# Mixer activations normalised in place, gates taken out of PSUM by ScalarE, and four of sixteen gate tiles as three products

## The chip, the cores and the metric

The kernel runs on one core of one Trainium2 chip. The metric is the device time of one execution in microseconds (us), as the median of several runs, and lower is better. In the profile the engines are PE (TensorE, the matrix unit), PEld (its weight loads), DVE (VectorE), ACT (ScalarE), POOL (GpSimd) and SP (the queue that issues most weight transfers). Every engine works through its own list of instructions in order; semaphores hold an instruction back until what it reads is there and what it overwrites has been read.

## The reference: what is computed

A trunk of two layers over 272 tokens (16 meta tokens and 256 others) with 1024 features, all in float32. Each layer is a mixer followed by a PEER block.

```python
h = _rmsnorm(x, mix_g)
z = h @ w_in                       # 1024 -> 3488 columns, the last 2048 of them gate logits
u = conv_in[..., :512] * sigmoid(conv_in[..., 512:])
u = silu(_layernorm(_causal_depthwise_conv(u, conv_w, conv_b)))     # 31 taps, 512 channels
y_conv = u @ w_conv_out
...                                # low-rank attention, 8 heads, chunk-causal: o
y_mla = o @ w_mla_out
gates = sigmoid(gate_logits)
merged = gates[..., :1024] * y_conv + gates[..., 1024:] * y_mla
h = x + merged @ w_out
```

The PEER block picks, for each token and each of 8 heads, 16 of 16384 experts by two top-16 searches, and adds `sum(gelu(u_e . h) * w_e * v_e)`. The second layer needs no outputs for the meta tokens, so most of its tiles are 256 columns wide where those of the first are 272.

## The kernel before

Activations lie transposed: features on the 128 partitions, tokens along the free dimension, 8 blocks of 128 features. Weights stream from HBM through a ring of four 1 MB buffers (`wraw`); each holds two tiles, and a tile is the 1024x128 weights of one output block. `next_w` goes one tile on and lets SP issue the transfer three buffers ahead; `peek_w(n)` looks at a tile that comes n tiles later. The order of the instructions on each engine is the order in which the Python code calls them. Nothing reorders them, so where a call stands in the program decides what it queues behind.

One mixer goes through these stages:

- **Input tiles.** `ztile` multiplies one tile of `w_in` with `xg`, the activations times the norm's gain. A tile is 8 float32 matmuls, which PE executes as 16 instructions. The factor `rs` of the RMS norm (one number per token) is not in `xg`; VectorE multiplies it into every result on its way out of PSUM. PSUM has three buffers named `z`, used in turn. Three tiles for the low-rank inputs and one for the rope keys come first, then eight for the convolution (loop over `c`, two tiles each, `za` and `zb`), then sixteen gate tiles (loop over `i`, 0 to 15).
- **Attention and convolution beside them.** `attention()` and `conv2()` are generators. Each loop advances them by `next(att)` and by `taps`, so that scores, softmax, transposes and mixes stand between the tiles on PE, and convolution taps (one VectorE instruction each) fill VectorE. The list `TAPS` says how many taps each gate tile brings. Channel block 0 has 21 of its 31 taps done by ScalarE and added up by POOL transfers.
- **Gates.** VectorE writes `z * rs` into `g0` or `g1` (L792). ScalarE applies the sigmoid in place later (L787), once the last exponential of the softmax is behind (`vt["exp"]`), which saves changes of ScalarE's function table.
- **LayerNorm.** When all taps are done, `layernorm()` is created and advanced by two steps a tile: two sums over PE, a reciprocal square root of eleven VectorE instructions, a sigmoid and a scaling on ScalarE for each of four blocks (L723, L724), then the products `u`.
- **Output tiles as three products.** The matrices `w_mla`, `w_conv`, `w_out` and part of `wq` are multiplied in another number format (float32r). ScalarE rounds a weight tile to a high part (`high`, L666), VectorE subtracts it from the weights to get a low part (`low`, L676), and `three` multiplies high x high, low x high and high x low: three instructions for each of 8 blocks, 24 a tile. `half_tile` makes the two halves of a tile of `w_mla` or `w_conv` (12 instructions each). The high and low parts reuse buffers that the mixer no longer needs: `wuq`, `seln` with `upad`, `kh`, `acc` with `sqa`, chosen by the part's number in `high`.
- **Merge and output.** `merge` multiplies the conv halves with their gates, adds the attention halves, and splits the sum in a high and a low part (`xh`, `xl`); eight tiles of `w_out` follow, then the sixteen tiles of `wq`, and the PEER block.

In the stage between, the tile numbers are: gate tiles 0 to 15, then parts 0 to 3 (the four tiles of `w_mla`), 4 to 7 (`w_conv`), 8 to 15 (`w_out`).

Of the kernel before, what the change touches and what calls it, by code (L numbers as in the profile page):

```python
# [20 lines left out]
T = 272  # L21
# [5 lines left out]
TAPS = [4, 4, 7, 7] + [9] * 12  # L27
KD = 21
SCALE = 96 ** -0.5
# [6 lines left out]
        "kh", "wuq", "seln", "upad", "acc", "sqa", "g0", "g1"}  # L36
# [13 lines left out]
def trunk_kernel(ctx: ExitStack, tc: tile.TileContext, a: dict, out: bass.AP, dbg=None, stop=None):  # L50
# [146 lines left out]
    for l in range(NL):  # L197
# [8 lines left out]
        rpool = rp.enter_context(tc.tile_pool(name=f"route{l}", bufs=1, side="right"))  # L206
# [28 lines left out]
        wuq = mp.tile([128, 2, 8 * 128], F32, name="wuq")  # L235
        wuk = mp.tile([128, 512], F32, name="wuk")
        wuv = mp.tile([128, 512], F32, name="wuv")
        qh, kh = pp.tile([128, 8, T], F32, name="xh"), mp.tile([128, 8, T], F32, name="kh")
        rope = mp.tile([128, T], F32, name="rope")
# [28 lines left out]
        nc.sync.dma_start(wuq, a["w_uq"][l])  # L268
# [37 lines left out]
        cq = mp.tile([128, 3, T], F32, name="cq")  # L306
# [14 lines left out]
        def attention():  # L321
# [15 lines left out]
            def qhead(h):  # L337
                pq = aps()
                for c in range(2):
                    mm(pq[:, :TQ], wuq[:, c, h * 128:(h + 1) * 128], cq[:, c, t0:], c == 0, c == 1)  # L340
# [229 lines left out]
            for x in range(11):  # L570
                p = x // 2
                if x % 2 == 0:
# [7 lines left out]
                    if p < 4:  # L580
                        softmax(p, ps)
                    yield
                else:
# [64 lines left out]

        def high(i, n):

            w_ = peek_w(n)
            x = {19: 3, 21: 4, 23: 1, 25: 2}.get(i, i % 3)
            if x == 0:
                t_ = mp.tile([128, 2, 1024], F32, name="wuq")
                hi, lo = t_[:, 0], t_[:, 1]
            elif x == 1:
                hi = mp.tile([128, 1024], F32, name="seln")
                lo = mp.tile([128, 1208], F32, name="upad")[:, 0:1024]
            elif i == 2 or x > 2:
                t_ = mp.tile([128, 8 * T], F32, name="kh" if x < 4 else "sq", tag="kh" if x < 4 else "sq")  # L660
                hi, lo = t_[:, 0:1024], t_[:, 1024:2048]
            else:
                hi = mp.tile([128, 4 * T], F32, name="acc")[:, 0:1024]
                lo = mp.tile([128, 4 * T], F32, name="sqa")[:, 0:1024]
            parts[i] = hi.bitcast(F32R), lo.bitcast(F32R), w_
            S.activation(parts[i][0], w_, AF.Copy)  # L666
            if i > 20:
                S.activation(parts[i][1], w_, AF.Copy, scale=-1.0)

        def low(i):  # L670

            hi, lo, w_ = parts[i]
            if i > 20:
# [874 lines left out]
```

## Time and profile before

| | |
|---|---|
| median of 3 runs | 1734.21 us (1732.22 to 1735.2) |
| profiled execution, its own time | 1733.18 us |
| its span, first to last instruction | 1731.4 us |
| PE busy | 1694.2 us (98% of the span), 11995 matmuls |
| DVE, ACT, POOL busy | 1148.1, 559.4, 306.5 us |
| mixer of layer 1 up to its last merge product | from the start to about 193 us |
| mixer of layer 2 | begins at 884.94 us |

A row of the timeline gives start, duration, engine, line, operation, output and inputs, shapes and a count, and in brackets an idle time before it with what ended it. A row with a count runs from the start of its first to the end of its last instruction; because matmuls are pipelined, a row's end overlaps the next row's start, and the distance from start to start is what a stretch takes. The list of waits gives the total, the number and the longest. A window row gives the busy time and, in brackets, the number of instructions of each engine, then the clock granted to PE (PEclk, 1.00 is full), the share of the transfer engines and GB/s. Line numbers up to the first changed line agree in both kernels; later ones of the changed kernel are higher.

### The profile page before, as it was taken

What the parts mean: (1) busy time and instruction counts of PE and PEld (TensorE: products, weight loads), DVE (VectorE), ACT (ScalarE), POOL (GpSimd) and SP (SyncE); (2) the same over time, 40 slices, a digit from 0 to 9 for tenths busy, and PEclk for the clock granted to TensorE, in tenths of its full rate; (3) what the DMA queues carried; (4) which work ended last, traced back from release to release, by engine and by line L of the source; (5) the groups of instructions that cost most, each with busy time, mean ns of one, the idle gap of its engine ahead of it and who ended that gap; (6) DMA issues with size and microseconds to landing.
All of it is one profiled execution on the core that took longest, in us unless ns stands there. A gap on an engine that the chain in (4) does not pass through costs nothing.

```text
span 1731.4 us, 30489 instructions
## 1 busy us (share of the span) xinstructions
PE 1694.2 (98%) x11995; PEld 1603.0 (93%) x11995; DVE 1148.1 (66%) x2987; ACT 559.4 (32%) x1596; POOL 306.5 (18%) x352
## 2 busy tenths in 40 slices
PE   9998999999999999999999989999999999999998
PEld 7677999989999999999986879999999999999998
DVE  6686888887888544443456868897888885333332
ACT  3455633434554111000024546333355441000000
POOL 0000022222112222233200100212221113222120
PEclk9999999999999999999999999999999999999999
DMA  6353686999999999999962546969999999999995
GB/s 238 108 146 122 219 266 238 369 382 418 420 420 416 421 421 421 421 420 416 418 251 98 134 131 232 288 273 365 396 425 424 424 418 415 389 387 391 397 391 206
DMA packets 85231, 568.50 MB, mean 328 GB/s; under 512 B 9560, under 2 KB 14872, under 8 KB 17624
## 3 DMA queue, kind: packets, MB, share of 16 engines
q1 hardware_dynamic: 49488, 338.54, 49.5%
q0 software_dynamic: 34880, 227.41, 33.9%
q8 instruction: 94, 1.54, 0.4%
q10 hardware_dynamic: 720, 0.60, 0.1%
q14 instruction: 49, 0.40, 0.1%
HBM read 556.18 MB, written 1.05 MB: 322 GB/s over the span
## 4 chain that ended last, share of the span: by engine, by line
PE 75%; issue 9%; DMA 8%; DVE 4%; POOL 2%; ACT 2%; POOLq 0%; SPq 0%; ACTq 0%; DVEq 0%
PE po L58 27%; PE z L58 20%; PE A L58 20%; DMA wraw<-vn 6%; PE aps L58 4%; DMA gb<-uv,iww 2%; POOL gb L1314 2%; PE wp L58 1%; PE sc L58 1%; PE xp L58 0%; DVE gb L1339 0%; DVE va L1325 0%; DVE upad L676 0%; DVE rq_w L179 0%; DVE rq_w L178 0%
## 5 line engine op out<-in xcount | busy, mean ns | idle before, releaser
L58 PE MATMUL A<-xh,wraw 128*128 128x160 f32 x3776 | 534.8, 301 | 1.2 <-ACT idxT L944 1.2
L58 PEld LDWEIGHTS A<-xh,wraw 128*128 128x128 f32 x3776 | 517.7, 191 | 1.6 <-issue 1.6
L1339 DVE SCALAR_TENSOR_TENSOR gb<-gb,xr 128x1024 f32<-128x1024 f32 x208 | 254.5, 1223 | 397.1 <-DMA gb<-uv,iww 396.7
L1314 POOL DMA_INDIRECT gb<-uv,iww x208 | 223.7, 1076 | 526.5 <-DVE va L1325 377.0
L58 PE MATMUL po<-Xh,wraw 128*128 128x160 f32 x2080 | 286.9, 300 | 4.1 <-DMA wraw<-vn 3.4
L58 PEld LDWEIGHTS po<-Xh,wraw 128*128 128x128 f32 x2080 | 283.1, 190 | 6.7 <-DMA wraw<-vn 5.4
L58 PE MATMUL po<-X,wraw 128*128 128x160 f32 x2016 | 277.8, 300 | 4.7 <-DMA wraw<-vn 2.5
L58 PEld LDWEIGHTS po<-X,wraw 128*128 128x128 f32 x2016 | 274.3, 190 | 7.7 <-DMA wraw<-vn 5.1
L58 PE MATMUL z<-xg,wraw 128*128 128x272 f32 (+2 forms) x1152 | 268.7, 391 | 0.0
L1325 DVE SCALAR_TENSOR_TENSOR va<-gb,am,va 128x1024 f32<-128x1024 f32 x203 | 259.6, 1279 | 4.0 <-ACT am L1350 3.7
L58 PEld LDWEIGHTS z<-xg,wraw 128*128 128x128 f32 (+1 forms) x1152 | 211.5, 189 | 46.0 <-issue 7.6
L1349 ACT ACTIVATE am<-am 128x1 f32<-128x1 f32 x208 | 41.3, 199 | 591.3 <-DVE gb L1339 591.2
L1253 ACT ACTIVATE ohA<-ohE,wlo 128x128 f16<-128x128 f16 x320 | 105.2, 429 | 6.4 <-DVE ohE L1250 5.7
L1313 POOL COPY warm<-wraw 1x1 f32<-1x1 f32 x86 | 40.7, 473 | 320.8 <-DMA wraw<-vn 320.8
L626 DVE SCALAR_TENSOR_TENSOR acc<-upad,cols,acc 128x272 f32<-128x272 f32 (+1 forms) x198 | 84.2, 484 | 0.2
L1264 ACT ACTIVATE Xh<-wp 128x260 f32<-128x260 f32 (+18 forms) x80 | 25.0, 313 | 126.5 <-DVE Xh L1261 116.6
L1350 ACT ACTIVATE am<-am,iww 128x1 f32<-128x1 f32 x208 | 61.3, 295 | 6.8
L1250 DVE TENSOR_TENSOR ohE<-ioh,idxT 128x512 f16<-128x512 f16 x160 | 60.1, 416 | 0.0
L638 POOL DMA_DIRECT2D part<-cp x12 | 13.2, 1102 | 249.4 <-ACT cp L635 249.4
L58 PE MATMUL wp<-ohE,ohA 128*128 128x128 f16 x640 | 51.4, 219 | 2.5 <-DVE ohA L1251 2.5
L58 PEld LDWEIGHTS <-ohA 128*128 128x128 f16 x640 | 43.3, 97 | 7.8 <-DVE ohA L1251 3.2
L58 PE MATMUL A<-xh,we 128*128 128x160 f32 x320 | 45.3, 299 | 0.0
(401 smaller groups left out, 1750.2 us busy)
## 6 DMA issues: line engine op xcount, KB each, us to landing
wraw<-vn SPq DMA_DIRECT2D x128, 1024.0 KB, 10.6
wraw<-u SPq DMA_DIRECT2D x118, 1024.0 KB, 10.3
wraw<-w_in SPq DMA_DIRECT2D x27, 1024.0 KB, 6.2
wraw<-wq SPq DMA_DIRECT2D x16, 1024.0 KB, 5.0
we<-u SPq DMA_DIRECT2D x10, 1024.0 KB, 8.8
wraw<-w_out SPq DMA_DIRECT2D x8, 1024.0 KB, 5.3
wraw<-w_mla SPq DMA_DIRECT2D x4, 1024.0 KB, 4.7
wraw<-w_conv SPq DMA_DIRECT2D x4, 1024.0 KB, 4.8
```

Source lines behind the costliest of these rows:

```text
L58: PE.matmul(o, l, r, start=start, stop=stop, skip_group_check=True)
L626: V.scalar_tensor_tensor(acc[:, c, t0:], u_, weight(c, k), acc[:, c, t0:], op0=OP.mult, op1=OP.add)
L638: G.dma_start(part[:, :, t0:], u_[:, :, t0:], accum_op=OP.add)
L1250: V.tensor_tensor(E[q], ioh[:, None].to_broadcast(full), pairs(q, b), op=OP.is_equal)
L1253: S.activation(A_[1][:, t // 2, :, t % 2], E[0][:, t // 2, :, t % 2], AF.Copy, scale=wlo[:, 4 * b + t:4 * b + t + 1])
L1264: S.activation(x_, p[:, :, a:b].rearrange("p t j -> p j t"), AF.Copy, scale=1.0 / WS)
L1313: G.tensor_copy(warm[0:1], state["w"][0:1, 0:1])
L1314: G.indirect_dma_start(out=g_, out_offset=None, in_=a[f"uv{l}"], in_offset=bass.IndirectOffsetOnAxis(ap=iww[i].bitcast(I32)[:, m // 16, 0, ...
L1325: V.scalar_tensor_tensor(vac[i], r, m_, vac[i], op0=OP.mult, op1=OP.add)
L1339: V.scalar_tensor_tensor(u_, u_, 1.0, xrs[i], op0=OP.mult, op1=OP.mult, accum_out=m_)
L1349: S.activation(m_, m_, AF.Gelu_apprx_tanh)
L1350: S.activation(m_, m_, AF.Copy, scale=iww[i][:, m // 16, 1, m % 16:m % 16 + 1])
```

## The change

Six things change in the mixer of each layer.

1. Between the two tiles of `c == 2`, VectorE multiplies `rs` into all eight blocks of `xg`, in place. From then on no result needs the factor: `zb` of block 2 goes straight to ScalarE's sigmoid, `za` of block 3 is read in PSUM by the product with the gate, and the sixteen gate tiles have no VectorE instruction.
2. ScalarE takes each gate out of PSUM: with the sigmoid at once if the last exponential is behind, otherwise as a copy whose sigmoid comes later from the list `todo`. `vt["exp"]` is set where the last softmax is issued, two tiles sooner.
3. `xg` is split into a high part `xnh` (ScalarE) and a low part `xnl` (VectorE), and gate tiles 12 to 15 (`TPG`) become three products. Their weight parts are `g12` to `g15`.
4. The parts of `w_mla` are prepared sooner: 0 at gate tile 13, 1 at tile 14, 2 and 3 at tile 15, and 4 and 5 after the first two half tiles. `kinds` lays out the buffers; `wuq` is split into `wq0` and `wq1`, and the buffer `xh`, free between the scores and the merge, is used too.
5. The taps are spread otherwise (`TAPS`), and the LayerNorm advances by 2, 4, 0 and 1 steps at the tiles after its creation, all between the two attention steps and what follows.
6. Small weights and `cq` share one buffer `un`, which `xnl` takes over; the pool of the routing is opened after the mixer.

```diff
-TAPS = [4, 4, 7, 7] + [9] * 12
+TAPS = [6, 6, 7, 8] + [8] * 12
+TPG = (12, 13, 14, 15)
...
+        kinds = {"g12": ("wq0", "x0"), "g13": ("wq1", "x1"), "g14": "s", "g15": "k", 0: "w", 1: "x", 2: "s", 3: "k",
+                 19: "k", 21: "q", 23: "s", 25: "a", 27: "w"}
...
+            x = kinds.get(i) or "was"[(i - 4) % 3]
...
             za = ztile(0)
             next(att, None)
             next(att, None)
+            if c == 2:
+                for k in range(8):
+                    V.tensor_mul(xg[:, k], xg[:, k], rs)
             zb = ztile(0)
...
-            V.tensor_mul(bz, zb, rs)
-            V.tensor_mul(az, za, rs)
-            S.activation(bz, bz, AF.Sigmoid)
+            if c < 2:
+                V.tensor_mul(bz, zb, rs)
+            if c < 3:
+                V.tensor_mul(az, za, rs)
+            S.activation(bz, bz if c < 2 else zb, AF.Sigmoid)
             next(att, None)
-            V.tensor_mul(upad[:, c, KW - 1:], az, bz)
-            taps((0, 0, 8, 4)[c], 2 if c >= 1 else 0, (1, 2, 3)[:max(c, 1)])
+            V.tensor_mul(upad[:, c, KW - 1:], az if c < 3 else za, bz)
+            if c == 2:
+                xnh = big("uk", [8, T], F32R)
+                xnl = mp.tile([128, 8, T], F32, name="un").bitcast(F32R)
+                for k in range(8):
+                    S.activation(xnh[:, k, t0:], xg[:, k, t0:], AF.Copy)
+                    V.tensor_tensor(xnl[:, k, t0:], xg[:, k, t0:], xnh[:, k, t0:].bitcast(F32), op=OP.subtract)
+            taps((0, 0, 8, 6)[c], 2 if c >= 1 else 0, (1, 2, 3)[:max(c, 1)])
...
         for i in range(16):
-            z = ztile(t0)
-            V.tensor_mul(gt[i // 8][:, i % 8, t0:], z, rs[:, t0:])
+            if i in TPG:
+                next_w()
+                z = zp.tile([128, 512], F32, name="z", bufs=3)[:, :TQ]
+                three(f"g{i}", z, (xnh, xnl), 0, range(8), 0, 7)
+            else:
+                z = ztile(t0)
+            ex = "exp" in vt
+            S.activation(gt[i // 8][:, i % 8, t0:], z, AF.Sigmoid if ex else AF.Copy)
+            if not ex:
+                todo.append(i)
+            new = [f"g{i + 2}"] if i + 2 in TPG else []
+            ns = [1] if new else []
+            for j in {13: (0,), 14: (1,), 15: (2, 3)}.get(i, ()):
+                new.append(j)
+                ns.append(15 - i + j)
+            for j, n in zip(new, ns):
+                high(j, n)
+            if i == 13:
+                for j in new:
+                    low(j)
+                new = []
...
-                next(ln, None)
                 next(att, None)
-                next(ln, None)
                 next(att, None)
-            if "exp" in vt:
-                gates(min(i + 1, ng[0] + 2))
-            if i == 14:
-                high(0, 1)
-                low(0)
-        gates(16)
-        high(1, 1)
+                for _ in range((2, 4, 0, 1)[lnk]):
+                    next(ln, None)
+                lnk += 1
+            for j in new:
+                low(j)
+            if ex:
+                gates(1)
...
-        low(1)
-        high(2, 2)
-        low(2)
         for i in range(4):
             ps = half_tile(i, oo)
-            if i == 2:
+            if i == 1:
                 run_all(ln)
-            if i < 3:
-                high(i + 3, 2)
-                low(i + 3)
+            if i < 2:
+                high(i + 4, 3)
             next(ln, None)
             for f in range(2):
                 V.tensor_mul(gt[1][:, 2 * i + f, t0:], gt[1][:, 2 * i + f, t0:], ps[f])
             next(ln, None)
-        run_all(ln)
+            if i < 2:
+                low(i + 4)
+            gates(2 if i < 2 else 4)
```

How the instructions stand now is shown at three places of the first layer. The first is ScalarE's list from the LayerNorm's last sigmoid (L723, L724) to the first products of `u` (L729). L666 is `high`, into the buffer named at its left. Before:

```order
L723 ACTIVATE sqa<-acc,cols_61 128x272
L724 ACTIVATE acc<-acc,cols_61 128x272
L787 ACTIVATE g_596<-g_596 128x272 x6
L666 ACTIVATE seln<-wraw 128x1024
L666 ACTIVATE kh<-wraw 128x1024
L666 ACTIVATE wuq<-wraw 128x1024
L729 ACTIVATE uk<-acc 128x272 x4
```

and now (L825 takes a gate out of PSUM, L814 is the later sigmoid, L676 is `high`, L733 and L734 are the LayerNorm's sigmoid and scaling):

```order
L825 ACTIVATE g_616<-z 128x272
L676 ACTIVATE kh<-wraw 128x1024
L676 ACTIVATE wq_1232<-wraw 128x1024
L814 ACTIVATE g_615<-g_615 128x272
L825 ACTIVATE g_616<-z 128x272
L676 ACTIVATE xh<-wraw 128x1024
L814 ACTIVATE g_615<-g_615 128x272
L825 ACTIVATE g_616<-z 128x272
L676 ACTIVATE seln<-wraw 128x1024
L676 ACTIVATE kh<-wraw 128x1024
L733 ACTIVATE sqa<-acc,cols_61 128x272
L734 ACTIVATE acc<-acc,cols_61 128x272
```

The high parts of the attention tiles stood behind the LayerNorm's eight instructions and six gate sigmoids; they now stand ahead of all of these.

The second place is VectorE's list at the end of the convolution (L626 are taps, L644 adds ScalarE's part, L686 is `low`, L713 and L716 begin the LayerNorm). This stretch now reads:

```order
L686 TENSOR_TENSOR xh<-wraw,wq_1080 128x1024
L626 SCALAR_TENSOR_TENSOR acc<-upad,cols_61,acc 128x272 x4
L531 TENSOR_TENSOR sq<-aps,sq 128x256
L626 SCALAR_TENSOR_TENSOR acc<-upad,cols_61,acc 128x272 x2
L644 TENSOR_TENSOR acc<-acc,part 128x272 x3
L686 TENSOR_TENSOR xh<-wraw,wq_1133 128x1024
L713 TENSOR_SCALAR kr<-aps 128x272
L716 TENSOR_TENSOR acc<-acc,kr 128x272 x4
L686 TENSOR_TENSOR upad<-wraw,seln 128x1024
L686 TENSOR_TENSOR kh<-wraw,kh 128x1024
L686 TENSOR_TENSOR wq_1233<-wraw,wq_1232 128x1024
L723 TENSOR_SCALAR rq_x<-aps 128x272
```

Here the low parts of the four gate tiles and of part 0 have come in: one ahead of the last taps, one behind the convolution, three between the LayerNorm's two halves. The two gate results of the stretch that VectorE took out of PSUM (L792) are gone.

The third place is VectorE's list where the LayerNorm ends and the conv products begin. L830, now L870, multiplies an attention half with its gate and so frees a PSUM buffer. Before:

```order
L720 TENSOR_TENSOR acc<-acc,rq_yl 128x272 x4
L676 TENSOR_TENSOR upad<-wraw,seln 128x1024
L676 TENSOR_TENSOR kh<-wraw,kh 128x1024
L676 TENSOR_TENSOR wuq<-wraw,wuq 128x1024
L728 TENSOR_TENSOR acc<-acc,sqa 128x272 x4
L731 TENSOR_TENSOR uk<-acc,uk 128x272 x4
L830 TENSOR_TENSOR g_596<-g_596,z 128x272
```

and now:

```order
L730 TENSOR_TENSOR acc<-acc,rq_yl 128x272 x4
L686 TENSOR_TENSOR upad<-wraw,seln 128x1024
L686 TENSOR_TENSOR kh<-wraw,kh 128x1024
L870 TENSOR_TENSOR g_616<-g_616,z 128x272
L870 TENSOR_TENSOR g_616<-g_616,aps 128x272
L738 TENSOR_TENSOR acc<-acc,sqa 128x272 x4
L741 TENSOR_TENSOR uk<-acc,uk 128x272 x4
L686 TENSOR_TENSOR wq_1366<-wraw,wq_1365 128x1024
L870 TENSOR_TENSOR g_616<-g_616,z 128x272
L870 TENSOR_TENSOR g_616<-g_616,aps 128x272
L686 TENSOR_TENSOR sqa<-wraw,acc 128x1024
```

The gating of the first half tile moved ahead of the LayerNorm's end, that of the second stays behind it and behind the low part of the first conv tile.

More of the change, by code (lines that the diff above doesn't have):

```diff
@@ L35 @@
 MIXQ = {"xg", "sq", "uk", "qr", "rq_w", "rq_x", "rq_ym", "tkw0", "tkw1", "tkw2", "sk", "scs", "qm",
-        "kh", "wuq", "seln", "upad", "acc", "sqa", "g0", "g1"}
+        "kh", "wq0", "wq1", "seln", "upad", "acc", "sqa", "g0", "g1"}
 GB = 4
@@ L234, in trunk_kernel @@
         xg, sq = big("xg", [8, T]), big("sq", [8, T])
-        wuq = mp.tile([128, 2, 8 * 128], F32, name="wuq")
-        wuk = mp.tile([128, 512], F32, name="wuk")
-        wuv = mp.tile([128, 512], F32, name="wuv")
+        wuq = [mp.tile([128, 1024], F32, name=f"wq{x}") for x in range(2)]
+        un = mp.tile([128, 8 * T], F32, name="un")
+        wuk, wuv, rope = un[:, 0:512], un[:, 512:1024], un[:, 1024:1024 + T]
+        cq = un[:, 1024 + T:1024 + 4 * T].rearrange("p (c t) -> p c t", c=3)
         qh, kh = pp.tile([128, 8, T], F32, name="xh"), mp.tile([128, 8, T], F32, name="kh")
-        rope = mp.tile([128, T], F32, name="rope")
         seln = mp.tile([128, 2, 128], F32, name="seln")
@@ L267, in trunk_kernel @@
             nc.sync.dma_start(cols[1], a["cols"][1])
-        nc.sync.dma_start(wuq, a["w_uq"][l])
+        for x in range(2):
+            nc.sync.dma_start(wuq[x], a["w_uq"][l, :, x])
         nc.sync.dma_start(rope[64:128], a["rope"])
@@ L339, in qhead @@
                 for c in range(2):
-                    mm(pq[:, :TQ], wuq[:, c, h * 128:(h + 1) * 128], cq[:, c, t0:], c == 0, c == 1)
+                    mm(pq[:, :TQ], wuq[c][:, h * 128:(h + 1) * 128], cq[:, c, t0:], c == 0, c == 1)
                 S.activation(qh[0:64, h, t0:], pq[0:64, :TQ], AF.Copy, scale=gqk)
@@ L581, in attention @@
                         softmax(p, ps)
+                    if p == 3:
+                        vt["exp"] = True
                     yield
@@ L782, in trunk_kernel @@
         ng = [0]
+        todo = []
         def gates(n):
-            while ng[0] < n:
-                g_ = gt[ng[0] // 8][:, ng[0] % 8, t0:]
+            while n and todo:
+                n -= 1
+                k = max(todo, key=lambda k_: (k_ // 8, -k_))
+                todo.remove(k)
+                g_ = gt[k // 8][:, k % 8, t0:]
                 S.activation(g_, g_, AF.Sigmoid)
-                ng[0] += 1
+        lnk = 0
         for i in range(16):
-            z = ztile(t0)
-            V.tensor_mul(gt[i // 8][:, i % 8, t0:], z, rs[:, t0:])
+            if i in TPG:
+                next_w()
+                z = zp.tile([128, 512], F32, name="z", bufs=3)[:, :TQ]
+                three(f"g{i}", z, (xnh, xnl), 0, range(8), 0, 7)
+            else:
+                z = ztile(t0)
[14 more added lines that the diff above has]
+                new = []
             if ln is None:
```

37 lines of the change are left out of this document (20 added, 17 removed).

## The prediction

> **What bounds the kernel now.** I read the page first, then the list of PE's waits, then PE, ScalarE and VectorE in order of time where a mixer ends. The page:
>
> ```profile
> PE 1694.2 (98%) x11995; PEld 1603.0 (93%) x11995; DVE 1148.1 (66%) x2987; ACT 559.4 (32%) x1596; POOL 306.5 (18%) x352
> ```
>
> PE is the bound, so the change can only win by giving PE fewer instructions, or where PE waits or runs slowly. PE's waits, with total, number and longest:
>
> ```profile
> PE z L58 <- ACT seln L666: 10.4, 2, 5.2
> PE z L58 <- DVE upad L676: 1.8, 3, 0.7
> PE z L58 <- DVE wuq L676: 1.3, 2, 0.7
> ```
>
> The largest comes once a layer: PE wants the high part of attention tile 1. The place in the first layer:
>
> ```profile
> 135.30 3.94 PE L58 MATMUL z<-xg,wraw 128*128 128x272 f32 x16
> 139.07 2.00 PE L58 MATMUL aps<-acc,ones 128*128 128x272 f32 x8
> 140.90 3.83 PE L58 MATMUL z<-xg,wraw 128*128 128x272 f32 x16
> 144.57 2.00 PE L58 MATMUL aps<-sqa,ones 128*128 128x272 f32 x8
> 146.40 7.50 PE L58 MATMUL z<-xg,wraw 128*128 128x272 f32 x32
> 153.54 0.49 PE L58 MATMUL z<-sq,wuq 128*128 128x272 f32 x1
> 163.00 0.59 PE L58 MATMUL z<-sq,seln 128*128 128x272 f32 x1 [5.21 <-ACT seln L666]
> 169.03 1.68 PE L58 MATMUL z<-sq,kh 128*128 128x272 f32 x12
> 175.08 0.29 PE L58 MATMUL z<-uk,seln 128*128 128x272 f32 x1
> 191.64 0.28 PE L58 MATMUL z<-xh,acc 128*128 128x272 f32 x1
> ...
> 155.37 0.62 ACT L723 ACTIVATE sqa<-acc,cols 128x272 f32<-128x272 f32 x1 [8.96 <-DVE acc L720]
> 159.47 0.61 ACT L724 ACTIVATE acc<-acc,cols 128x272 f32<-128x272 f32 x1
> 161.91 1.04 ACT L666 ACTIVATE seln<-wraw 128x1024 fp32r<-128x1024 f32 x1
> ...
> 160.00:170.00 10.00, 6.33 (x32) 6.03 (x33) 7.01 (x13) 7.05 (x15) 0.00 (x0) 0.66 0.47 174
> ```
>
> The high part stands on ScalarE behind the LayerNorm's eight instructions, 155.37 to 160.08, and six sigmoids. Those are late because the LayerNorm is. PE then stands still, and restarts at a granted clock of 0.66.
>
> From 169.03 to 175.08 parts 2 and 3 take 6.05 us for 48 instructions, 0.126 each, and so 3.02 a tile. Parts 0 and 1 take 169.03 - 153.54 = 15.49 instead: **9.4 us lost** in layer 1. In layer 2:
>
> ```profile
> 1025.13 0.47 PE L58 MATMUL z<-sq,wuq 128*128 128x256 f32 x1
> 1039.83 0.40 PE L58 MATMUL z<-sq,kh 128*128 128x256 f32 x2
> 1051.21 1.59 PE L58 MATMUL z<-uk,wuq 128*128 128x256 f32 x12
> 1052.64 1.57 PE L58 MATMUL aps<-uk,wuq 128*128 128x256 f32 x12
> ...
> 1013.23:1016.68 3.45, 3.45 (x17) 3.04 (x16) 1.85 (x5) 2.33 (x8) 0.00 (x0) 1.00 0.02 5
> ```
>
> Twelve instructions take 1.42 (1052.64 - 1051.21, rounded), a tile 2.84; 14.70 - 5.68 leaves **9.0 us lost**.
>
> **The change, part by part.**
>
> *Three products.* A float32 gate tile takes 144.57 - 140.90 = 3.67 us, and 3.45 in layer 2 (the window above). As three products it takes 3.02 and 2.84. Four tiles a layer: 4 x 0.65 + 4 x 0.61 = **5.0 us less on PE**. The per-instruction time holds for any weights and inputs of this shape, so I take it whole; at least 0 if the low parts are late, which the stalls below count. [...]
>
> *Preparation sooner.* The two losses, 9.4 + 9.0 = 18.4 us, go if nothing else is late. I followed the new lists on the clock of before, with these durations:
>
> ```profile
> L845 ACT ACTIVATE xh<-az 128x272 fp32r<-128x272 f32 x8 | 3.3, 427 | 4.5 <-DVE az L844 4.4
> L844 DVE TENSOR_TENSOR az<-az,g 128x272 f32<-128x272 f32 x8 | 3.5, 442 | 0.3
> ...
> 130.57 3.79 DVE L626 SCALAR_TENSOR_TENSOR acc<-upad,cols,acc 128x272 f32<-128x272 f32 x9
> 137.44 1.38 DVE L644 TENSOR_TENSOR acc<-acc,part 128x272 f32<-128x272 f32 x3
> 146.60 0.44 DVE L713 TENSOR_SCALAR rq_x<-aps 128x272 f32<-128x272 f32 x1 [1.39 <-PE aps L58]
> 150.27 0.44 DVE L792 TENSOR_TENSOR g<-z,rq_ym 128x272 f32<-128x272 f32 x1 [1.12 <-PE z L58]
> 153.00 0.44 DVE L180 SCALAR_TENSOR_TENSOR rq_yl<-rq_w,rq_yl 128x272 f32<-128x272 f32 x1
> 162.98 1.23 DVE L676 TENSOR_TENSOR upad<-wraw,seln 128x1024 fp32r<-128x1024 f32 x1 [6.66 <-ACT seln L666]
> 164.12 1.22 DVE L676 TENSOR_TENSOR kh<-wraw,kh 128x1024 fp32r<-128x1024 f32 x1
> 166.86 1.49 ACT L729 ACTIVATE uk<-acc 128x272 fp32r<-128x272 f32 x4 [2.02 <-DVE acc L728]
> 176.37 1.23 DVE L676 TENSOR_TENSOR wuq<-wraw,wuq 128x1024 fp32r<-128x1024 f32 x1 [0.66 <-ACT wuq L666]
> 190.65 1.02 DVE L848 TENSOR_TENSOR kh<-az,xh 128x272 fp32r<-128x272 f32 x2
> ```
>
> A low part costs VectorE 1.14 (164.12 - 162.98), a tap 0.41, a high part 1.04 of ScalarE (161.91 above), a copy or gate 0.43, the LayerNorm's inverse root 153.44 - 146.60 less the wait and the gate within, so 5.4.
>
> - VectorE: eight taps from 130.6 to 133.9, the low part for gate tile 12 to 135.05, just ahead of its start at 135.30. Then four taps, the attention output, two taps, three adds: to 139.2. PE ends tile 12 at 138.3 and waits for the LayerNorm's first sum: **0.9 us**.
> - Sum to 141.1, tile 13 to 144.1, second sum to 145.9, tile 14 to 148.95, tile 15 to 151.95. VectorE meanwhile: low parts 13, 14, 15 and 0 by 147.95, the inverse root by 153.35, low part 1 by 154.5. Part 0 starts on PE at 151.95, part 1 at 155.0: both ready. Low parts 2 and 3 follow the four products L730, at 157.05 and 158.2; PE wants them at 158.0 and 161.0. The 5.2 us wait is gone.
> - Next late is `u`: ScalarE's eight instructions run 155.0 to 159.7, then a sigmoid, high part 4, and the four copies, to 162.45; VectorE's differences end at 162.9, low part 4 at 164.05. PE is done with part 3 at 164.05, but its buffer `z` is freed by the gating behind low part 4, at 164.45: **0.5 us**.
> - VectorE then does low part 5, four gatings, low part 6 from 167.3. From low part 6 to the last difference before took 191.67 - 176.37 = 15.3 us with nearly no gap, so it ends at 182.6 now. PE, from 164.55, has four tiles and 36 output products, and wants the last blocks at 181.2: **1.4 us**. At this place before was 191.64 and is now 182.5: **9.1 us gained** in layer 1.
>
> Layer 2 by the same list and its shorter rows: waits of 0.3, 0.15, 1.3 and 1.2 us; gain 4 x 0.61 + 9.0 - 2.95 = 8.5.
>
> *Normalising in place and the split of `xg`.* VectorE adds 2 x 8 instructions of 0.37 to 0.44 us a layer and loses 19 (one, two and sixteen). ScalarE adds 8 copies of 0.43 and 8 more gate passes. Whether PE waits for the first eight:
>
> ```profile
> 57.49 0.44 DVE L410 SCALAR_TENSOR_TENSOR ss<-aps,mq 128x272 f32<-128x272 f32 x1 [3.57 <-PE aps L58]
> 59.40 3.93 PE L58 MATMUL z<-xg,wraw 128*128 128x272 f32 x16
> ```
>
> They start at 57.9 behind L410; the first block is there at 58.3, the next every 0.37, while PE starts on them at 59.40 and takes 0.46 a block. Cost 0; without that cover it would be the whole eight, 3.3 us a layer. The subtractions fall where VectorE is idle:
>
> ```profile
> 60.00:80.00 20.00, 20.00 (x97) 15.72 (x99) 14.10 (x47) 5.27 (x11) 1.11 (x1) 1.00 0.41 127
> 100.00:120.00 20.00, 20.00 (x119) 15.27 (x118) 17.28 (x49) 10.98 (x34) 1.17 (x2) 1.00 0.46 137
> ```
>
> 14.1 plus about 5 is still under 20, and later VectorE has 0.44 less a tile. ScalarE's 11 of 20 rises by under 2. Cost 0. A gate waits on ScalarE behind what that engine still has to do, and PE comes back to the same `z` buffer three tiles later, at least 3 x 3.67 = 11 us; behind it stand that tile's exponentials and `cp` passes, which the same tile on PE precedes.
>
> *Transfers and the rest.* A `wraw` buffer of gates 12 to 15 is now freed by VectorE's low part, by 140.4 and 146.8. A buffer lands in 5.3 us:
>
> ```profile
> wraw<-w_out SPq DMA_DIRECT2D x8, 1024.0 KB, 5.3
> ```
>
> Its next readers come after 160. The lists of PEER are unchanged, so it follows as it was.
>
> **Sum**: 5.0 + 18.4 - (0.9 + 0.5 + 1.4) - (0.3 + 0.15 + 1.3 + 1.2) = 17.6 us. From the profiled 1733.18 us, whose span of 1731.4 lies inside it, that gives 1715.6. The median shown is 1.0 above the profiled one, so I predict **1716 us**. The unknown costs bound it: with no new wait at all the gain is 23.4, 1711; if each replayed step of VectorE and ScalarE ran late by as much again as the waits found, 5.8 us more, 1722.
>
> **Rivals.**
>
> - *VectorE becomes the bound from tile 12 on.* It carries the low parts of eight tiles in 25 us. If its list runs 4 us late at the LayerNorm, PE waits 4 us a layer more ahead of the `u` products, 8 in all; by the row at 160 a wait of 5.2 slows the clock after it, costing about 2.3 more (169.03 - 163.00 = 6.03, less a wait of 0.7 and the 3.02 of full clock). Then 17.6 - 8 - 4.6 leaves 5, about 1728. For it: 182.6 against 181.2 shows VectorE last already. Against: a wait of PE hands VectorE time, and its gate products are gone. [...]
> - *The change doesn't shift PEER.* If the weight stream ran ahead in the time won, part of the next layer's lead would be gone. Its ring holds four buffers, full in both kernels, so I give it little; half of layer 1's gain lost is 4.5, 1720.5, inside the range.
> - *Gates queue on ScalarE.* If a gate stands behind an exponential that waits for VectorE, for longer than the two further `z` buffers last, PE stops at the next tile. It decides from a delay of some 9 us (two tiles and a sum, 135.30 to 144.57). Each gate tile would then cost the excess; at 1 us for 32 tiles that is 32 - 17.6 = 14 slower, 1748. Against: the chain from score to exponential lies within one tile in the trace, 10.98 of 20 busy.
>
> **How the numbers follow.** Chances: forecast 0.72, VectorE's bound 0.15, lost lead 0.06, gates queueing 0.03, and 0.04 for something smaller that leaves 1731 to 1738. The forecast's own range is 1711 to 1722. To hold 8 in 10 and part of the second case, the range goes from 1710 to 1726. This kernel's measurement tells apart some 0.2%, 3.5 us: faster than 1730.7 takes the first three cases, 0.93, within it 0.04, slower 0.03.
>
> **What would show it.** Gate tiles 12 to 15 at 3.0 us start to start on PE; no wait of PE above 2 us before the merge and no window of the mixers under 0.95 clock; a wait on `acc` at the first sum, one ahead of the first `u` product, one at the last blocks of the first two output tiles; the output tiles 9 us earlier in layer 1 and 17 to 18 in layer 2; PEER of the same length. Wrong would be: PE waiting among gate tiles 0 to 11 (ScalarE's gates or the in-place products), one wait over 3 us at the LayerNorm, or PEER longer.

## The result, and the profile after

The changed kernel takes **1715.62 us** (median of four, 1714.13 to 1717.95), where the kernel before, run beside it, takes 1734.7. The ratio is 0.9893, 95% interval 0.9876 to 0.991: 1.1% faster. 1716 had been forecast.

The profiled execution took 1717.95 us, with a span of 1715.8. The page after, its row of busy times:

```profile
PE 1687.0 (98%) x12059; PEld 1599.0 (93%) x12059; DVE 1153.1 (67%) x2989; ACT 577.7 (34%) x1636; POOL 310.4 (18%) x352
```

PE still is the bound, with 7 us less. In the list of PE's waits (total, number, longest) the 10.4 us for the high part 1 are gone. What is new in the mixers is short, and all of it is for VectorE (the few for ScalarE, 0.2 to 0.6 us each, were there before):

```profile
PE wp L59 <- DVE ohA L1294: 3.8, 1, 3.8
PE z L59 <- DVE upad L686: 1.1, 2, 0.6
PE z L59 <- DVE g L870: 0.9, 1, 0.9
PE aps L59 <- DVE acc L644: 0.8, 1, 0.8
PE z L59 <- DVE wq L686: 0.7, 2, 0.4
```

(The first of these rows lies in PEER, and is taken up with the first experiment.) PE in order of time in layer 1 after, from a row near the start to the first product of PEER (start, duration, engine, line, operation, tiles, shape, count, and in brackets the wait ahead with what ended it):

```profile
56.66 0.63 PE L59 MATMUL aps<-sk,strip 128*16 128x272 f32 x2 [0.46 <-ACT sk L392]
135.13 0.39 PE L59 MATMUL z<-uk,wq 128*128 128x272 f32 x1
139.18 2.07 PE L59 MATMUL aps<-acc,ones 128*128 128x272 f32 x8 [0.76 <-DVE acc L644]
151.96 1.67 PE L59 MATMUL z<-sq,wq 128*128 128x272 f32 x12
158.01 0.29 PE L59 MATMUL z<-sq,seln 128*128 128x272 f32 x1
161.03 1.68 PE L59 MATMUL z<-sq,kh 128*128 128x272 f32 x12
164.37 1.74 PE L59 MATMUL z<-uk,wq 128*128 128x272 f32 x12
179.46 0.39 PE L59 MATMUL z<-xh,upad 128*128 128x272 f32 x1 [0.42 <-DVE upad L686]
181.69 0.28 PE L59 MATMUL z<-xh,acc 128*128 128x272 f32 x1
266.30 8.93 PE L59 MATMUL A<-xh,wraw 128*128 128x160 f32 x64 [0.64 <-ACT idxT L987]
```

Parts 0 and 1 take 158.01 - 151.96 = 6.05 us, what parts 2 and 3 took before: the stall of 9.4 us is gone whole. No window of one microsecond in the two mixers is below full clock any more, where before six of them in each mixer had a clock of 0.50; the stretch of the old stall, by the windows view after (length, busy time and instructions of PE, PEld, DVE, ACT and POOL, granted clock, DMA share, GB/s):

```profile
151.00:164.00 13.00, 13.00 (x105) 12.99 (x104) 11.90 (x24) 10.69 (x19) 0.00 (x0) 1.00 0.47 166
```

Layer 2, the first product of the mixer, then gate tile 12, the first `u` product, the second output tile's low part, and the first product of PEER:

```profile
877.67 8.64 PE L59 MATMUL z<-xg,wraw 128*128 128x272 f32 x37
1000.67 0.39 PE L59 MATMUL z<-uk,wq 128*128 128x256 f32 x1
1028.28 1.67 PE L59 MATMUL z<-uk,wq 128*128 128x256 f32 x12 [0.91 <-DVE g L870]
1043.00 0.39 PE L59 MATMUL z<-xh,upad 128*128 128x256 f32 x1 [0.63 <-DVE upad L686]
1123.43 8.93 PE L59 MATMUL A<-xh,wraw 128*128 128x160 f32 x64 [0.58 <-ACT idxT L987]
```

The rows of before that answer to these:

```profile
56.82 0.63 PE L58 MATMUL aps<-sk,strip 128*16 128x272 f32 x2 [0.46 <-ACT sk L392]
275.97 8.93 PE L58 MATMUL A<-xh,wraw 128*128 128x160 f32 x64 [0.64 <-ACT idxT L944]
884.94 2.23 PE L58 MATMUL z<-xg,wraw 128*128 128x272 f32 x9
1007.94 3.72 PE L58 MATMUL z<-xg,wraw 128*128 128x256 f32 x16
1139.65 1.60 PE L58 MATMUL A<-xh,wraw 128*128 128x160 f32 x10 [0.58 <-ACT idxT L944]
```

Two lengths sum up a kernel better than its time. **Mixer 1** runs from the `aps<-sk,strip` row to the first row `A<-xh,wraw` (the start of the program is left out: in the runs below that row comes anywhere from 56.31 to 57.68 us). **Mixer 2** runs from the first `z<-xg,wraw` of layer 2 to the second `A<-xh,wraw`. Before: 275.97 - 56.82 = 219.15 and 1139.65 - 884.94 = 254.71. After: 266.30 - 56.66 = 209.64 and 1123.43 - 877.67 = 245.76. The change wins **9.51 and 8.95 us**, 18.5 in all; 17.6 had been forecast.

All runs, by these two lengths (each read from the same rows of its own trace), beside their medians and their ratios to the kernel before, which ran on the same chip each time:

| kernel | mixer 1 | mixer 2 | against the change | median | ratio to before, 95% |
|---|---|---|---|---|---|
| before | 219.15 | 254.71 | +18.5 | 1734.7 | |
| the change | 209.64 | 245.76 | | 1715.62 | 0.9893 (0.9876 to 0.991) |
| the change again | 209.64 | 245.74 | 0.0 | 1715.29 | 0.989 (0.9875 to 0.9905) |
| gates 12 to 15 float32 | 210.70 | 247.25 | +2.6 | 1717.88 | 0.9902 (0.9888 to 0.9916) |
| parts late | 216.78 | 252.15 | +13.5 | 1728.82 | 0.9961 (0.9949 to 0.9973) |
| gates by VectorE | 210.90 | 246.87 | +2.4 | 1717.3 | 0.9897 (0.9882 to 0.9911) |
| LayerNorm even | 210.55 | 247.96 | +3.1 | 1718.86 | 0.991 (0.9895 to 0.9925) |
| four low parts on GpSimd | 216.85 | 248.31 | +9.8 | 1724.6 | 0.994 (0.9926 to 0.9953) |
| six low parts on GpSimd | 220.87 | 252.02 | +17.5 | 1732.14 | 0.9989 (0.998 to 0.9998) |
| order at `u` | 209.03 | 245.15 | -1.2 | 1713.72 | 0.9878 (0.9861 to 0.9894) |
| order at `u`, taps earlier | 208.04 | 244.88 | -2.5 | 1713.14 | 0.9877 (0.9861 to 0.9894) |
| before, with filling products | 218.91 | 254.87 | +18.4 | 1732.47 | 0.9982 (0.9973 to 0.9991) |

The lengths of the change agree to 0.02 us between its two executions. That is one pair only, but a stretch that most of these kernels share, from the `sk` row to gate tile 12 of layer 1, is 78.47 or 78.48 us in nine of the twelve profiles. So tenths can be read from these lengths.

### The profile page after: what moved, and what is told of

It reads as the page before. It is cut to its first block, busy times and chain, and to the rows that moved or that the text cites. A ratio compares the mean times of both kernels' runs of the same rounds, so it can differ in the third digit from the quotient of the medians.

```text
span 1715.8 us, 30664 instructions
## 1 busy us (share of the span) xinstructions
PE 1687.0 (98%) x12059; PEld 1599.0 (93%) x12059; DVE 1153.1 (67%) x2989; ACT 577.7 (34%) x1636; POOL 310.4 (18%) x352
## 4 chain that ended last, share of the span: by engine, by line
PE 72%; DMA 13%; DVE 10%; ACT 2%; issue 2%; POOL 1%; SPq 0%; POOLq 0%; DVEq 0%; ACTq 0%
PE po L59 25%; PE A L59 23%; PE z L59 16%; DMA wraw<-vn 8%; DMA gb<-uv,iww 3%; PE aps L59 3%; PE wp L59 2%; DVE va L1368 1%; DVE gb L1382 1%; DMA wraw<-u 1%; PE sc L59 1%; DVE wq L686 1%; POOL gb L1357 1%; PE xp L59 0%; DVE ex L1073 0%
## 5 line engine op out<-in xcount | busy, mean ns | idle before, releaser
L1357 POOL DMA_INDIRECT gb<-uv,iww x208 | 227.4, 1093 | 505.8 <-DVE va L1368 362.2
L59 PE MATMUL z<-xg,wraw 128*128 128x272 f32 (+2 forms) x1024 | 238.9, 391 | 0.4 <-DMA wraw<-w_in 0.4
L59 PEld LDWEIGHTS z<-xg,wraw 128*128 128x128 f32 (+1 forms) x1024 | 187.2, 189 | 41.5 <-issue 6.6
L626 DVE SCALAR_TENSOR_TENSOR acc<-upad,cols,acc 128x272 f32<-128x272 f32 (+1 forms) x198 | 82.9, 485 | 0.2
```

The costliest lines, as they stand in the source:

```text
L59: PE.matmul(o, l, r, start=start, stop=stop, skip_group_check=True)
L626: V.scalar_tensor_tensor(acc[:, c, t0:], u_, weight(c, k), acc[:, c, t0:], op0=OP.mult, op1=OP.add)
L1357: G.indirect_dma_start(out=g_, out_offset=None, in_=a[f"uv{l}"], in_offset=bass.IndirectOffsetOnAxis(ap=iww[i].bitcast(I32)[:, m // 16, 0, ...
```

## The experiments

**The changed kernel once more.** In the first profile PEER of layer 1 ran from 266.30 to 877.67, 611.37 us, where before it took 884.94 - 275.97 = 608.97. That looked like the rival of the lost lead.

> The changed kernel once more, on the chip of the next three runs, so that they have a measure beside them. Every theory expects a ratio to the kernel before between 0.988 and 0.991. In the first profile of it the mixers start the next stage 18.6 us sooner in all (9.67 and 8.95), but the two PEER stages of layer 1 give 2.4 us back. If that is a property of the change (VectorE or the weight stream come out differently there), this profile shows PEER of layer 1 about 2.4 us longer than before again; if it differs from execution to execution, the figure will be another one here, and the rest of the page the same.

The second execution:

```profile
56.77 0.63 PE L59 MATMUL aps<-sk,strip 128*16 128x272 f32 x2 [0.46 <-ACT sk L392]
266.41 8.93 PE L59 MATMUL A<-xh,wraw 128*128 128x160 f32 x64 [0.64 <-ACT idxT L987]
875.40 2.91 PE L59 MATMUL z<-xg,wraw 128*128 128x272 f32 x12
1121.14 8.93 PE L59 MATMUL A<-xh,wraw 128*128 128x160 f32 x64 [0.58 <-ACT idxT L987]
```

PEER took 875.40 - 266.41 = 608.99, as before. The 2.4 us were not the change. The wait of 3.8 us for `ohA` was in the first execution alone; here the waits for `ohA` are 1.0 us in all, the longest 0.5. The largest such wait of all profiles, 4.7 us, stands in a kernel made from the one before (the filling products). Over the twelve profiles PEER of layer 1 takes 607.98 to 612.61 us, and the longest is that same kernel's. What makes PEER differ from one execution to the next was not looked into.

**The last four gate tiles as float32.**

```diff
-TPG = (12, 13, 14, 15)
+TPG = ()
```

> The changed kernel with gate tiles 12 to 15 of both mixers as float32 products again, so without the split of their weights (one high part on ScalarE and one low part on VectorE less for each of the four). The normalised activations are still split, and nobody uses the split for the gates. Theory A, that the waits which the change brought (0.8 at the first sum of the LayerNorm, 0.9 at the gating, 1.1 and 0.6 at the output tiles, some 2 to 2.5 us a layer) are there because VectorE is late with low parts: PE pays 5.0 us for the products, but gets back most of the waits, 3 to 4 us in two layers, so 1 to 2 us slower than the change. Theory B, that these waits come from elsewhere (the chain of the LayerNorm or the buffers): the full 5 us slower. The start to start of a gate tile 12 goes from about 3.0 back to 3.67 us in both.

(Two lines not shown let part 1 take the buffer `xh`, which in the change the gate parts take first.)

PE in this run in order of time: gate tile 12 and part 2 of layer 1, the first wait that is left behind tile 12 there, and tile 12 and part 2 of layer 2:

```profile
135.05 3.93 PE L59 MATMUL z<-xg,wraw 128*128 128x272 f32 x16
159.52 0.29 PE L59 MATMUL z<-sq,seln 128*128 128x272 f32 x1
180.43 0.39 PE L59 MATMUL z<-xh,upad 128*128 128x272 f32 x1 [0.25 <-DVE upad L688]
998.24 1.13 PE L59 MATMUL z<-xg,wraw 128*128 128x256 f32 x4
1021.27 0.28 PE L59 MATMUL z<-sq,seln 128*128 128x256 f32 x1
```

From tile 12 to part 2, both kernels free of other waits there, PE takes 159.52 - 135.05 = 24.47 us; the change takes 158.01 - 135.13 = 22.88, less its wait of 0.76, 22.12. So three products win PE **2.35** in layer 1. In layer 2 it is 1021.27 - 998.24 = 23.03 against 1021.53 - 1000.67 = 20.86 (the first product of part 2 after starts at 1021.53), **2.17**. Together 4.5 and not 5.0. Yet the mixers are only 2.6 longer: 1.9 us come back, since with the four low parts the waits at the first sum and ahead of `u` go, but for 0.3 in layer 2. The result lies between the two theories, nearer to A: about half of the 3.8 us of new waits is the price of these low parts, and the three products are worth 2.6 us net.

**The attention parts prepared late.**

```diff
-            for j in {13: (0,), 14: (1,), 15: (2, 3)}.get(i, ()):
+            for j in {14: (0,)}.get(i, ()):
...
+        high(1, 1)
         run_all(att)
...
+        low(1)
+        high(2, 2)
+        low(2)
...
```

> The changed kernel with the high and low parts of attention tiles 0 to 3 prepared at the places of the kernel before: tile 0 at gate tile 14, tile 1 on ScalarE behind the eight squares of the LayerNorm, tile 2 behind the first product, each later one three ahead. All else stays: the LayerNorm still has its taps earlier, and the last four gate tiles are three products. Theory A, that the stall of the kernel before was the order of ScalarE and VectorE: PE waits some 5 us for the high part 1 again, and runs at a granted clock near 0.66 after it, 5 to 8 us a layer, 10 to 16 in all, so about 1726 to 1732. Theory B, that the stall went because the LayerNorm is now sooner: under 2 us a layer, at most 1720.

PE in order of time at parts 0 and 1:

```profile
153.49 1.65 PE L59 MATMUL z<-sq,wq 128*128 128x272 f32 x11 [1.17 <-DVE wq L686]
159.93 0.59 PE L59 MATMUL z<-sq,xh 128*128 128x272 f32 x1 [3.27 <-ACT xh L676]
```

and the window behind them, the granted clock third from the end:

```profile
160.00:166.00 6.00, 5.33 (x22) 5.03 (x23) 6.00 (x11) 3.28 (x7) 0.00 (x0) 0.50 0.62 221
```

The wait for the high part and the half clock behind it are back, and with them 13.5 us of the 18.5. What is left, 5.0, is all that the rest of the change wins without the early parts, and the three products alone save PE 4.5. So by this sum the early LayerNorm and the gates on ScalarE win next to nothing without the early parts; the order of the parts carried the gain. Theory A holds.

**The LayerNorm in even steps**, the other half of that order:

```diff
-                for _ in range((2, 4, 0, 1)[lnk]):
+                for _ in range(2):
```

> The changed kernel with the LayerNorm issued two steps a gate tile through tiles 12 to 15, as in the kernel before, in place of two, four, none and one. The second sum, the squares and the inverse root then come behind the low parts of later tiles on VectorE. Theory A, that the early LayerNorm is needed beside the early parts: u is ready later, and PE's wait ahead of the u products grows from 0.9 to 2 to 5 us a layer, 3 to 8 in all, about 1719 to 1724. Theory B, that the early parts alone carried the gain: under 1 us in all.

PE at part 3 in both layers, and then the windows behind these two waits:

```profile
163.37 1.74 PE L59 MATMUL z<-sq,kh 128*128 128x272 f32 x12 [2.04 <-DVE g L870]
1025.52 1.88 PE L59 MATMUL z<-sq,kh 128*128 128x256 f32 x12 [2.61 <-DVE g L870]
```

```profile
165.00:170.00 5.00, 5.00 (x42) 5.00 (x42) 4.97 (x11) 0.33 (x1) 0.00 (x0) 1.00 0.47 152
1027.00:1030.00 3.00, 3.00 (x16) 3.00 (x16) 2.63 (x6) 0.09 (x1) 0.00 (x0) 0.50 0.13 22
```

The mixers are 3.1 us longer, inside theory A's range by its lower end. The place was another one: not the first `u` product, but part 3, whose buffer `z` is freed by the first gating; with even steps that gating stands behind all of the LayerNorm. Early parts and early LayerNorm thus belong together, but unequally: 13.5 and 3.1. (What one loses by taking single pieces back does not add up to the gain: 13.5, 3.1, 2.6 for the three products and 2.4 for the gates below make 21.6, more than 18.5, so the pieces lean on each other.)

**All gates taken out by VectorE.**

```diff
-            S.activation(gt[i // 8][:, i % 8, t0:], z, AF.Sigmoid if ex else AF.Copy)
-            if not ex:
-                todo.append(i)
+            V.tensor_copy(gt[i // 8][:, i % 8, t0:], z)
+            todo.append(i)
```

> The changed kernel with every gate taken out of PSUM by VectorE with a copy, and its sigmoid on ScalarE later from SBUF, where the change lets ScalarE take them all. It puts 16 copies of 0.43 us a layer back on VectorE, 4 of them from tile 12 on, where VectorE was last. Theory A (VectorE is the last engine there): its list is 1.7 us later at the LayerNorm, and the wait of PE at the first sum or ahead of the u products grows by 1 to 2 us a layer, 2 to 4 in all. Theory B (there is cover left, since the waits of one place hand VectorE time for the next): under 1 us in all. The rival that gates queue on ScalarE would show as a gain here.

The mixers are 2.4 us longer, theory A. Of the 1.26 in layer 1, 0.5 comes ahead of gate tile 12, 0.35 is the wait at the first sum, 1.11 where it was 0.76 (PE in order of time), and the rest comes behind it:

```profile
141.04 2.07 PE L59 MATMUL aps<-acc,ones 128*128 128x272 f32 x8 [1.11 <-DVE acc L644]
```

So the move of the gates to ScalarE, which the prediction had put at 0, is worth 2.4 us in this kernel: 16 copies of 0.43 us a layer find only part of their time in VectorE's idle time.

**Four low parts on GpSimd, and six.** With VectorE last, the plain thought was to give its work to the idle GpSimd.

```diff
-                V.tensor_tensor(lo, w_, hi.bitcast(F32), op=OP.subtract)
+                (G if i in ("g12", "g13", "g14", 0) else V).tensor_tensor(lo, w_, hi.bitcast(F32), op=OP.subtract)
```

> The changed kernel with the low parts of gate tiles 12, 13 and 14 and of attention tile 0 on GpSimd in place of VectorE, in both mixers. On VectorE such a low part takes 1.14 us; GpSimd's product of 272 columns took 1.03, so an estimate for 1024 columns is 3.9 us, and GpSimd has nothing else there. Each of the four has 3.9 us between its high part and PE's use of it. Theory A, that VectorE's low parts are what PE still waits for: 4.6 us of VectorE's list a layer is gone, the wait of 0.76 at the first sum goes, those ahead of u and at the output tiles shrink, 1.5 to 2 us a layer, 3 to 4 in all, so about 1712. Theory B, that GpSimd is slower than the estimate, or slows VectorE while both run: no gain, or a new wait of PE for a low part, up to 4 us slower.

> As the run with four low parts on GpSimd, and the low parts of attention tiles 1 and 2 there too. By the estimate of 3.9 us a low part, part 1 is done at about 154.6 of layer 1, just ahead of PE's use at 155.0, and part 2 at about 158.6, 0.6 behind it. Theory A (the estimate holds): VectorE wins another 2.3 us a layer, but PE pays 0.6 to 1 us a layer at part 2; total within 1 us of the run with four. Theory B (GpSimd slower than 3.9): PE waits 1 us more for every 0.5 us by which it is slower, since two stand in a row, and the run is over 2 us slower than the one with four.

(With six, parts 1 and 2 are in the list too.) Both are far slower than the change. GpSimd and VectorE in the run with four, what PE then waits for, and two taps in the change itself for comparison:

```profile
129.92 2.36 POOL L686 TENSOR_TENSOR xh<-wraw,wq 128x1024 fp32r<-128x1024 f32 x1 [3.00 <-ACT wq L676]
135.39 3.98 POOL L686 TENSOR_TENSOR xh<-wraw,wq 128x1024 fp32r<-128x1024 f32 x1 [3.11 <-ACT wq L676]
140.22 2.42 POOL L686 TENSOR_TENSOR upad<-wraw,seln 128x1024 fp32r<-128x1024 f32 x1 [0.85 <-ACT seln L676]
...
130.51 6.61 DVE L626 SCALAR_TENSOR_TENSOR acc<-upad,cols,acc 128x272 f32<-128x272 f32 x12
137.38 2.71 DVE L626 SCALAR_TENSOR_TENSOR acc<-upad,cols,acc 128x272 f32<-128x272 f32 x2
140.01 3.40 DVE L644 TENSOR_TENSOR acc<-acc,part 128x272 f32<-128x272 f32 x3
154.01 2.03 DVE L176 TENSOR_SCALAR rq_w<-rq_x 128x272 int32<-128x272 int32 x1
...
143.56 3.96 PE L59 MATMUL aps<-acc,ones 128*128 128x272 f32 x8 [5.03 <-DVE acc L644]
...
136.82 0.91 DVE L626 SCALAR_TENSOR_TENSOR acc<-upad,cols,acc 128x272 f32<-128x272 f32 x2
```

GpSimd itself is faster than estimated, 2.4 us. But VectorE's instructions take longer meanwhile: two taps take 2.71 where they take 0.91 in the change, three adds 3.40 where they took 1.38 before, and the instruction at 154.01, beside a fourth low part on GpSimd, takes 2.03 where it takes 0.30 in the change. The other way round, the GpSimd instruction at 135.39 takes 3.98 while VectorE's taps are under way. So the 1.14 us which VectorE saves by a low part cost it 1.6 to 2.0, most of the 2.4 us that GpSimd works on it; why the two engines hold each other up was not shown. Ahead of the first sum of layer 1 this happens three times: twelve taps take 6.61 where an estimate from eight in the change, 3.38, gives 5.0, then the two taps and the three adds. That is 1.6 + 1.8 + 2.0 = 5.4 us, less the 1.14 of the one low part that VectorE no longer does there 4.3, and PE's wait grows by 5.03 - 0.76 = 4.27. Half clock follows (0.50 from about 142 to 148). In layer 2 the same wait is 1.40. This is theory B, in its second form. With six it is worse by another 7.7, where theory A had put it within 1; that is the time of its theory B, but not its reason, since GpSimd was faster than 3.9 us: PE's new waits there, 3.57 and 3.61, are for VectorE's gating.

**The kernel before, its wait filled.**

```diff
+            if i == 1:
+                p = aps()
+                for _ in range(20):
+                    mm(p[:, 0:128], ones, ones, True, True)
```

> The kernel before, with 20 more products of ones by ones (128 columns, float32, results unused) on PE between attention tiles 0 and 1 of both mixers, where PE waits 5.2 us for the high part 1. Nothing else changes: the wait has the same end. Theory A, that the idle time itself lowers the granted clock and that this is a part of the loss of its own (after its wait of 5.21 us part 1 took 6.03 us in layer 1, of which 0.7 is a further wait and 3.02 the products): PE stays at a clock of 1.00 in the windows after the wait, and the next part begins 2 to 2.5 us sooner, 4 to 5 us faster in two layers, about 1730. Theory B, that the products after the wait are slow for another reason (their inputs or the low part come late): the same time, or up to 2 us slower from the products added.

PE from the added products to part 1, and the windows behind them:

```profile
157.43 4.63 PE L58 MATMUL aps<-ones 128*128 128x128 f32 x40
162.80 0.39 PE L58 MATMUL z<-sq,seln 128*128 128x272 f32 x1 [0.75 <-ACT seln L666]
164.06 0.40 PE L58 MATMUL z<-sq,upad 128*128 128x272 f32 x1 [0.87 <-DVE upad L676]
```

```profile
162.00:165.00 3.00, 1.38 (x9) 1.12 (x9) 2.22 (x2) 2.65 (x3) 0.00 (x0) 1.00 0.02 5
165.00:169.00 4.00, 4.00 (x22) 4.00 (x21) 4.00 (x10) 1.75 (x5) 0.00 (x0) 0.57 0.96 354
```

The clock stays full through the filled wait (1.00 from 157 to 165), and then falls all the same, about 1 us after the work has resumed: the two short waits that are left, 0.75 and 0.87, stand ahead of it, and nothing longer. The mixers are 0.1 us shorter, so theory A's 4 to 5 did not come. The time is theory B's, but not its reason alone: the products were at half clock again. The measured time is 0.18% lower (0.9973 to 0.9991), and the rows of the mixers don't account for it; where it comes from stays open. Filling the long wait was no cure for the half clock while the short ones were left.

**VectorE's order at `u`.**

```diff
-            if i == 1:
-                run_all(ln)
-            if i < 2:
-                high(i + 4, 3)
-            next(ln, None)
+            if i == 0:
+                high(4, 3)
+                next(ln, None)
             for f in range(2):
                 V.tensor_mul(gt[1][:, 2 * i + f, t0:], gt[1][:, 2 * i + f, t0:], ps[f])
...
+            if i == 1:
+                run_all(ln)
+                high(5, 3)
+                low(4)
+                low(5)
```

(A step of the LayerNorm also ends ahead of its differences, so that the gatings can stand between.)

> The changed kernel with VectorE's order at the u products mended and nothing else: the two gatings of attention tile 1 stand between the sigmoid's products and the differences of u (where VectorE was idle for 0.97 us of layer 1), and low part 4 behind the differences, in place of differences, low part 4, gatings. The z buffer of tile 1 is then free some 2.5 us sooner. Theory A, that the wait ahead of the u products was the gating standing behind low part 4: the wait of 0.9 us in layer 2 and the 0.3 of layer 1 go, up to 1.2 us in all. Theory B, that part 4 is then late instead, or that VectorE, last at the output tiles, takes it back there: within 0.3 us.

```profile
164.13 1.67 PE L59 MATMUL z<-uk,wq 128*128 128x272 f32 x12
```

This is PE's first `u` product of layer 1: it comes 3.02 us behind part 3 (161.11), without a wait. In layer 2 0.35, for the low part, is left of 0.91. The mixers are 1.2 us shorter, theory A.

**That, and four taps earlier.**

```diff
-TAPS = [6, 6, 7, 8] + [8] * 12
+TAPS = [6, 6, 7, 9, 9, 9, 9] + [8] * 9
```

> The run with the mended order at u, and four taps of the convolution earlier: gate tiles 3 to 6 take 9 taps each in place of 8, so that tile 11 has two left in place of six. Four taps are 1.6 us of VectorE. Theory A, that the wait of 0.76 at the LayerNorm's first sum stands behind VectorE's last taps: it goes, everything behind it moves up, and the mixers together are 2 to 3 us shorter than those of the change (512.1 us from the program's start to the first PEER and from the second mixer's start to the second PEER), about 1713. Theory B, that the earlier taps hold up the attention's steps on VectorE: PE waits among the gate tiles 3 to 7, 1 to 3 us longer.

The first sum in layer 1:

```profile
138.56 2.00 PE L59 MATMUL aps<-acc,ones 128*128 128x272 f32 x8
```

The wait there is gone, no wait came among the gate tiles, and the mixers are 2.5 us shorter than the change's: theory A. This is the fastest kernel here, 1713.14 us. By the times alone its ratio to before, 0.9877 (0.9861 to 0.9894), can't be told from the change's 0.989 (0.9875 to 0.9905); the rows of the mixers tell it.

## Why the prediction was right, step by step

- **The two stalls, 18.4 us.** Right, and the reason too: parts 0 and 1 take 6.05 us after, and with the parts late again the wait for ScalarE's high part and the half clock return (3.27 us, clock 0.50).
- **Three products, 5.0 us.** A little too high: PE does 4.5 us less (2.35 and 2.17). The row 144.57 - 140.90 = 3.67 was taken for all four float32 tiles, but two tiles in a row take 3.57 each (153.54 - 146.40 = 7.14), and the first instruction of a tile behind float32 work takes some 0.33 in place of 0.126 (141.00 to 141.33 in the second execution). Else the time of an instruction held for these weights and inputs too: gate tile 15, behind a tile of its own kind, takes 151.96 - 148.95 = 3.01 us. The net worth is 2.6, since the low parts cost waits; the prediction had those under the stalls.
- **The new waits, 2.8 and 2.95.** The larger ones were found at their places or next to them, two small ones of layer 2 (0.3 and 0.15) not at all, and together they are 3.8 in place of 5.75. The wait at the first sum: 0.76 for 0.9, and none in layer 2. Ahead of `u`: 164.37 - 161.03 - 3.02 = 0.3 for 0.5, and 0.91 for 1.3. At the output tiles the replay had the last blocks late by 1.4 and 1.2; it was the low parts of the second and third output tile, 0.42 and 0.30, then 0.63 and 0.44. VectorE's list ended a little sooner than replayed: its last difference at 181.99 for 182.6, and the output tiles' place on PE at 181.69 for 182.5. With 4.5 for the products these make 4.5 + 18.4 - 3.8 = 19.1; 0.4 of it is counted twice, since the slow first instruction at part 0 stands in the stall's 9.4 and 9.0 as well as in the products' 4.5. 18.7 is left, and 18.5 was measured. (That sum is rough: 0.44 of the waits stood in layer 2 before, too, and the restart behind a wait is not in it: the instruction at 179.46 takes 0.23 to the next one and not 0.126. By the starts of PE's rows alone, the change wins 10.85 and 11.03 from gate tile 12 to part 2, and loses 1.35 and 2.08 from there to PEER: 18.45.)
- **How near the sum came is in part luck.** The waits were put at 5.75 and measured 3.8; the products, put 0.5 too high, took part of that back. So 17.6 lies 0.9 from 18.5, where the waits alone were off by 2.0. (In the last step 1715.6 and 1.0 make 1716.6, not 1716; that changes nothing.)
- **Normalising in place, at 0.** No cost, as forecast: gate tile 12 starts 135.30 - 56.82 = 78.48 us behind the `sk` row before, and 135.13 - 56.66 = 78.47 after; in layer 2 1007.94 - 884.94 and 1000.67 - 877.67 are both 123.00. What VectorE wins by doing fewer of these products was not measured by itself.
- **Gates on ScalarE, at 0.** Right that they cost PE nothing; but left out was what VectorE wins by it. As copies they cost 2.4 us. The forecast contained this gain without naming it, since the replay had no gate products on VectorE from tile 12 on.
- **The rivals.** VectorE as the bound: it is the engine for which PE waits in every new row, but for 0.91 us at most and not for 4. Two experiments show how near the edge it is (even steps 2.0 and 2.6 us; GpSimd's help 5.0). The lost lead: not there, PEER takes 608.99 in the second execution against 608.97. Gates queueing: the reverse is true, by the run with VectorE's copies.
- **A row that the prediction overlooked.** The first rival takes the slower clock behind a wait from one row, the wait of 5.2 us. A shorter wait of the kernel before has it too: in PEER of layer 1, PE waits 2.47 us (at 374.43), and half clock follows (0.50 from 376.5 to 379.5). The forecast does not rest on it, since no wait in the mixers after is above 0.91.
- **The list of signs** held in the main: waits at `acc`, ahead of `u` and at the output tiles, none over 2 us, no slow window, PEER as long in the second execution. Two were off in detail: gate tiles 13 and 14 take 3.2 us and not 3.0 (140.88 to 144.11 and 145.74 to 148.95, each behind a float32 sum), and the waits at the output tiles stand at low parts, not at the last blocks.

Where it could have gone wrong is the range: it assumed that replayed steps come late together. A wait of PE gives VectorE as much time for the next place, so errors of such a list do not simply add; that is argued from the order of the work, no run tests it alone.

## What to carry to other kernels

When one engine stands in front of another's critical input, look for what is queued ahead of that input: eight LayerNorm instructions and six sigmoids ahead of one weight split cost 9 us a layer, and the new order brought back less than 4 us of waits in both. Replaying the new lists instruction by instruction with durations from the old trace gave the sum to 1 us of 18.5 and pointed to the places of most remaining waits; two small reorderings then took 2.5 us of them away. Judge small edits by the length of the stage in the trace, which repeated to 0.02 us here, where the time of one kernel wanders by 1 to 6 between executions.

## What the runs showed of the hardware that was not expected

- **The clock fell without one long gap ahead of it.** The two waits of 0.75 and 0.87 us, ended at 162.80 and 164.06, were all that stood ahead of a halved clock once the long wait was filled, in layer 2 too (0.71 and 0.88); one wait of 2.04 us was not followed by it (clock 1.00 from 165 to 170), one of 2.61 was (0.50 from 1027 to 1030). Nor does the length alone tell: at one place in PEER of layer 1, PE waits 2.47 and then 0.91 us before, ended at 374.43 and 375.78, and half clock follows; after, it waits 2.67 and 0.91 at the same place, ended at 364.96 and 366.31, and the clock stays at 1.00 until the next wait, of 3.83, ended at 380.16. By windows of half a microsecond the low stretch began up to 1.2 us after PE had resumed; it lasted some 3.4 us (about 165.3 to 168.7 here) or about twice that (159.7 to 166.5 with the parts late, by windows of one microsecond). In the three microseconds from 162 on, ahead of the fall at 165.3, PE was busy for 1.38. What decides when the clock falls was not shown.
- **GpSimd's subtractions and VectorE's work held each other up.** A low part of 2.4 us on GpSimd stretched what VectorE did beside it by 1.6 to 2.0 us, and one that began behind VectorE's taps took 3.98. In this kernel GpSimd was nearly idle in the mixers (in the change busy for 6.05 of the first 194 us) and still was no place to put this work.
